# A two-layer decoder step on one core: the first FFN product by Strassen's seven products, each FFN in two phases through DRAM

## The chip, the cores and the metric

The kernel runs on one core of one Trainium2 chip. The time is device microseconds of one execution. Lower is better. Three runs of the kernel before took 2004.39, 2007.34 and 2011.28 us, so the median is 2007.34 us.

## The reference

One inference step works on 1024 prompt tokens, 16 meta tokens ahead of them, and 8 sample tokens: 1048 columns of 1024 features, in float32. Layer 0 mixes by causal pooling, layer 1 by sliding-window attention. After each mixer stands a layer norm, then the ConvFFN, then a layer norm:

```python
gu = xs @ w_in                       # 1024 -> 2 x 2816: gate and up
g, u = gu[..., :D_FF], gu[..., D_FF:]
gp = concatenate([prefix, g], axis=1)
c = conv_b + sum(gp[:, k:k + S] * conv_w[k] for k in range(3))
h = silu(c) * u
return h @ w_out, gp[:, -2:]         # 2816 -> 1024
...
hp = layer_norm(ALPHA * hp + f_p, g, b)
```

## The kernel before

Features lie on the 128 partitions and tokens along the columns. The tokens come in three chunks of 280, 384 and 384 columns (in layer 1 the first chunk has 266 for the gate and 264 elsewhere, since most meta tokens are no longer needed). Every float32 operand of a product is split into a high part and a low part, `h` or `hi` and `l` or `lo`, and `mm3` (L115 to L122) adds three products of parts: hi by hi, hi by lo, lo by hi. A layer norm (`ln_steps`) ends by writing the two parts of its result: ScalarE writes the high part `xh`, and VectorE the low part `xl` at L233 (POOL at L222 for some tiles). `load_w` (L103 on) fetches a weight tile by a DMA on the SP queue, casts it on ScalarE (L111) and subtracts on POOL for the low part (L112).

The FFN (`ffn`) runs over 22 feature tiles f of the inner width. For each tile and each chunk `ffn1` makes the gate `pg` and the up value `pu` in one PSUM bank each, 24 matmuls a bank (8 feature tiles k times three parts). POOL, VectorE and ScalarE then make the convolution, the Silu, the product and the two parts of h, which stay in SBUF. After every second f, `ffn2` multiplies two h tiles with their output weights, 8 output tiles of 6 matmuls, and VectorE adds each bank to the accumulator `acc` (L420). `ffn2_last` does this for the last two tiles (L433, L441). Layer norms of early chunks run beside the products of later ones, both at the FFN's end and at its start, where the FFN of chunk 0 begins while chunk 2 is still in the mixer's norm.

The program is traced in source order; a scheduler orders each engine's instructions by priority and by when they are ready, and sets the waits. Six PSUM banks turn under the name "mm". The mean of a norm is a product with `ones` (L143, or L165 and L166 after sums on POOL and VectorE), the subtraction is L188, the scaling by gain and inverse deviation L224. In the pooling L326 adds a product to the sum; in the attention's output projection it is L762 and L764, where `pz` is the product of 12 matmuls for each half.

Of the kernel before, what the change touches and what calls it, by code (L numbers as in the profile page):

```python
# [13 lines left out]
P = 128  # L14
D = 1024
KT = D // P
SEQ = 1024
# [10 lines left out]
# prompt blocks (of 128 tokens) per chunk; the first chunk also carries the  # L28
# meta tokens and the sample tokens: columns [meta 16 | samples 8 | prompt]
# [6 lines left out]
# columns alive after the attention: [meta14 meta15 | samples 8 | prompt]  # L36
# [3 lines left out]
# packed per-partition constant columns  # L40
# [7 lines left out]
# constants of the first phase alone  # L48
# [9 lines left out]

@with_exitstack
def trunk_kernel(ctx: ExitStack, tc: tile.TileContext, ins: dict, outs: dict):  # L60
    nc = tc.nc
    pool = ctx.enter_context(tc.tile_pool(name="sb", bufs=1))
    psum = ctx.enter_context(tc.tile_pool(name="ps", bufs=1, space=bass.MemoryType.PSUM))

    def bank(name, tag="mm"):
        return psum.tile([P, 512], F32, tag=tag, bufs=6 if tag == "mm" else 2, name=name)

    def tmp(shape, name, dt=F32):
        return pool.tile(shape, dt, tag="tmp", bufs=8, name=name)

    def ltmp(shape, name, dt=F32):
        return pool.tile(shape, dt, tag="lt", bufs=5, name=name)

    def tiny(shape, name):
        return pool.tile(shape, F32, tag="tiny", bufs=6, name=name)

    def hslot(shape, name, dt=F32R):
        return pool.tile(shape, dt, tag="h", bufs=12, name=name)

    # ------------------------------------------------------------ constants  # L80
# [7 lines left out]
    cr = pool.tile([P, NF, NCH, 2], F32, name="carry")  # L88
    gs = pool.tile([P, NF, NS], F32, name="gs")
# [3 lines left out]

    def xh_tile(c, m, name, dt=F32R):
        return pool.tile([P, WX[c]], dt, tag=f"xh{c}_{m}", name=f"{name}{c}_{m}")

    xh = [[xh_tile(c, m, "xh") for m in range(KT)] for c in range(NCH)]
    xl = [pool.tile([P, KT, WX[c]], F32R, name=f"xl{c}") for c in range(NCH)]
# [4 lines left out]
    def load_w(src, name, tag="w", pieces=1, w=None):  # L103
        raw = pool.tile([P, 1024], F32, tag="raw", bufs=2, name=f"raw_{name}")
        nc.sync.dma_start(raw, src)
        if w is None:
            w = pool.tile([P, 2, 1024], F32R, tag=tag, bufs={"w": 4, "wo": 2}.get(tag, 1), name=f"w_{name}")
# [7 lines left out]
    def mm3(out, wts, movs):  # L115
        """out += sum_k w_k^T x_k over exact hi/lo parts (all but lo*lo)."""
# [859 lines left out]
```

## Time and profile before

| | us |
|---|---|
| median of three runs | 2007.34 |
| the runs | 2004.39, 2007.34, 2011.28 |
| span of the profiled execution | 2004.4 |
| TensorE busy in it (PE) | 1932.9 (96%), 12208 matmuls |
| VectorE (DVE) | 1263.3 (63%) |
| ScalarE (ACT) | 712.3 (36%) |
| POOL | 813.9 (41%) |
| DMA moved | 123.45 MB |

The durations that the profile gives for matmuls overlap, since matmuls are pipelined: a listed 0.33 us is the time of one from its start to its end, and the distance between starts is what a stream of them costs. PEclk is the granted TensorE clock as a share of full speed.

### The profile page before, as it was taken

The numbers are of one execution on the slowest core, as the hardware profiler recorded it, in microseconds if no ns is written. First come the engines' busy times: TensorE is split into PE (matmuls) and PEld (weight loads), VectorE is DVE, ScalarE is ACT, GpSimd is POOL, SyncE is SP. The second block draws the span as 40 slices with busy tenths as digits, with TensorE's granted clock in tenths as the row PEclk, the third lists the DMA queues.
The fourth block names the chain that finished last, engine by engine and source line by source line (L and its number), as shares of the span: only waits on it lengthen the run. The fifth ranks groups of instructions, "written<-read, shape, count | busy, mean of one in ns | idle before, by whom it ended". The sixth has DMA issues, their size and how long they took to land. (4 is left out here: it accounts for less than half of the span.)

```text
span 2004.4 us, 31349 instructions
## 1 busy us (share of the span) xinstructions
PE 1932.9 (96%) x12208; PEld 1896.3 (95%) x12208; DVE 1263.3 (63%) x2367; ACT 712.3 (36%) x1585; POOL 813.9 (41%) x880
## 2 busy tenths in 40 slices
PE   6899999999999999899999989999999999999997
PEld 4699999999999999889999988999999999999996
DVE  7977545454544456887989896675445454544566
ACT  2452122112211221476778784512122112212234
POOL 6752334214321432653464657533143224322333
PEclk9899999999999999999999999999999999999998
DMA  5201111101110111314343322011011011101102
GB/s 194 78 22 43 53 54 63 43 22 64 64 37 27 64 53 34 30 49 148 107 132 102 109 81 85 32 51 55 33 64 55 31 42 63 54 32 43 64 23 65
DMA packets 50422, 123.45 MB, mean 62 GB/s; under 512 B 11481, under 2 KB 25489, under 8 KB 50217
## 3 DMA queue, kind: packets, MB, share of 16 engines
q1 hardware_dynamic: 50272, 121.44, 19.6%
q8 instruction: 96, 1.57, 0.3%
q14 instruction: 54, 0.43, 0.1%
HBM read 108.29 MB, written 7.54 MB: 58 GB/s over the span
## 5 line engine op out<-in xcount | busy, mean ns | idle before, releaser
L112 POOL TENSOR_TENSOR w_wo<-raw_wo,w_wo 128x512 fp32r<-128x512 f32 (+1 forms) x92 | 169.3, 1859 | 550.9 <-ACT w_wo L111 548.0
L121 PE MATMUL pg<-xl,w_g 128*128 128x384 f32 (+2 forms) x1056 | 337.4, 319 | 0.0
L121 PE MATMUL pu<-xl,w_u 128*128 128x384 f32 (+2 forms) x1056 | 336.6, 319 | 0.0
L420 DVE TENSOR_TENSOR acc<-acc,po 128x384 f32<-128x384 f32 (+2 forms) x432 | 222.1, 515 | 173.8 <-PE po L122 170.9
L121 PE MATMUL po<-h,w_wo 128*128 128x384 f32 (+2 forms) x960 | 305.9, 319 | 0.0
L120 PE MATMUL po<-h,w_wo 128*128 128x384 f32 (+2 forms) x960 | 305.7, 318 | 0.0
L122 PE MATMUL po<-h,w_wo 128*128 128x384 f32 (+2 forms) x960 | 305.6, 318 | 0.0
L111 ACT CAST w_wo<-raw_wo 128x512 fp32r<-128x512 f32 (+1 forms) x92 | 71.6, 822 | 422.4 <-PE po L122 417.6
L402 DVE TENSOR_TENSOR h<-c,h 128x280 fp32r<-128x280 f32 (+2 forms) x132 | 147.7, 1119 | 88.3 <-ACT h L401 87.7
L392 POOL TENSOR_SCALAR c<-g,cols 128x384 f32<-128x384 f32 (+1 forms) x110 | 80.2, 729 | 294.6 <-issue 281.6
L121 PEld LDWEIGHTS pg<-xl,w_g 128*128 128x128 f32 x1056 | 198.8, 188 | 0.1
L121 PEld LDWEIGHTS pu<-xl,w_u 128*128 128x128 f32 x1056 | 198.3, 188 | 0.0
L393 DVE SCALAR_TENSOR_TENSOR c<-g,cols,c 128x384 f32<-128x384 f32 (+1 forms) x110 | 67.8, 616 | 194.4 <-POOL c L392 194.4
L122 PEld LDWEIGHTS po<-h,w_wo 128*128 128x128 f32 x960 | 180.4, 188 | 0.0
L120 PEld LDWEIGHTS po<-h,w_wo 128*128 128x128 f32 x960 | 180.3, 188 | 0.0
L121 PEld LDWEIGHTS po<-h,w_wo 128*128 128x128 f32 x960 | 180.1, 188 | 0.0
L398 ACT ACTIVATE c<-c 128x280 f32<-128x280 f32 (+2 forms) x132 | 65.1, 493 | 312.4 <-DVE c L394 277.5
L120 PE MATMUL pg<-xh,w_g 128*128 128x384 f32 (+1 forms) x528 | 170.1, 322 | 0.0
L122 PE MATMUL pg<-xh,w_g 128*128 128x384 f32 (+1 forms) x528 | 169.1, 320 | 0.0
L120 PE MATMUL pu<-xh,w_u 128*128 128x384 f32 (+1 forms) x528 | 168.9, 320 | 0.0
L122 PE MATMUL pu<-xh,w_u 128*128 128x384 f32 (+1 forms) x528 | 168.8, 320 | 0.0
L120 PE MATMUL pg<-xa,w_g 128*128 128x384 f32 (+1 forms) x528 | 168.6, 319 | 0.0
(270 smaller groups left out, 4673.5 us busy)
## 6 DMA issues: line engine op xcount, KB each, us to landing
raw_g<-in_win SPq DMA_DIRECT2D x44, 512.0 KB, 3.5
raw_u<-in_win SPq DMA_DIRECT2D x44, 512.0 KB, 3.5
raw_wo<-in_wout SPq DMA_DIRECT2D x44, 512.0 KB, 3.5
raw_wq<-in_wq SPq DMA_DIRECT2D x24, 512.0 KB, 3.5
raw_wo<-in_wo SPq DMA_DIRECT2D x24, 512.0 KB, 3.6
q<-q SPq DMA_DIRECT2D x64, 96.0 KB, 2.1
praw<-in_xq SPq DMA_DIRECT2D x8, 400.0 KB, 5.4
out_yT<-acc SPq DMA_DIRECT2D x8, 384.0 KB, 2.5
```

The costliest lines, as they stand in the source:

```text
L111: nc.scalar.copy(w[:, 0, s], raw[:, s])
L112: nc.gpsimd.tensor_tensor(w[:, 1, s], raw[:, s], r32(w[:, 0, s]), ALU.subtract)
L120: nc.tensor.matmul(out, lhsT=wh, rhs=mh, start=(k == 0), stop=False)
L121: nc.tensor.matmul(out, lhsT=wh, rhs=ml, start=False, stop=False)
L122: nc.tensor.matmul(out, lhsT=wl, rhs=mh, start=False, stop=(k == n - 1))
L392: nc.gpsimd.tensor_scalar(cc, g[:, 0:n], w0, b, ALU.mult, ALU.add)
L393: nc.vector.scalar_tensor_tensor(cc, g[:, 1:1 + n], w1, cc, ALU.mult, ALU.add)
L398: nc.scalar.activation(ct, ct, AF.Silu)
L402: nc.vector.tensor_tensor(ht[:, 1, :], ct, r32(ht[:, 0, :]), ALU.subtract)
L420: nc.vector.tensor_tensor(a, a, ps, ALU.add)
```

## The change

Strassen's scheme (in the form with seven products and fifteen additions) takes the first FFN product. The weight block is two tiles f by two halves of the 1024 features, the token block two feature halves by two column quarters. Seven products of sums replace eight. `ffn_a` builds the seven token operands X once for each of two column halves b (quarters of 262 columns in layer 0, and of 260 in layer 1 with six dummy columns), each split into two parts. For each of 22 sets (11 pairs of f, gate then up) `prep` loads two weight tiles, makes four sums, and splits seven operands. Three accumulators of two banks each, B, A and C, take the products; the running values of B are copied out by ScalarE between the products that are added to it. Gate rows G, the convolution C and up rows U hold all tokens of a pair; h is written to DRAM. `ffn_b` then reads h and the residual back and does the second product in groups of three tiles f, with the layer norms behind it. All chunks' inputs are needed before the first set is complete. Memory is handed over in phases: pools are closed and opened between the stages. The attention's norm writes its scaled result to the new buffers of layer 1 in place of the parts of x.

```diff
-    def ffn(L, first_w):
...
-        win = {0: first_w, 1: load_in(1), 2: load_in(2, "wo")}
-        for c in range(NCH):
-            for f in range(3):
-                ffn1(f, c, *win[f])
...
+    def ffn_a(L, Y):
+        def build_x(b):
+            q = 2 * b * w
+            B = {(i, j): Y[i][:, :, q + j * w:q + (j + 1) * w] for i in range(2) for j in range(2)}
+            def parts(n, srcs, pool_lo):
+                t = lt.tile([P, 2, 4, w], F32R, tag=f"x{b}{n}", name=f"x{L}_{b}{n}")
+                for h, src in enumerate(srcs):
...
+                    nc.scalar.copy(t[:, 0, ks], src)
+                    (nc.gpsimd if pool_lo else nc.vector).tensor_tensor(t[:, 1, ks], src, r32(t[:, 0, ks]), ALU.subtract)
...
+        def prep(s):
+            raw = lt.tile([P, 2, 1024], F32, tag="raw2", bufs=2, name=f"raw{L}_{s}")
+            nc.sync.dma_start(raw, ins["win"][L, f:f + 2].rearrange("a p c -> p a c"))
+            def parts(n, src, eng):
+                t = lt.tile([P, 2, 512], F32R, tag="ws", bufs=8, name=f"w{L}_{s}{n}")
+                nc.scalar.copy(t[:, 0], src)
+                eng.tensor_tensor(t[:, 1], src, r32(t[:, 0]), ALU.subtract)
...
+            parts("11", A[0, 0], nc.gpsimd)
+            parts("12", A[0, 1], nc.vector)
+            nc.vector.tensor_tensor(st["s1"], A[1, 0], A[1, 1], ALU.add)
+            nc.vector.tensor_tensor(st["s2"], st["s1"], A[0, 0], ALU.subtract)
+            parts("s2", st["s2"], nc.gpsimd)
...
+        def prod(out, W, n, xn, start, stop, bs=(0, 1)):
+            for b in bs:
+                o = out[:, b, :w]
+                for k in range(4):
+                    nc.tensor.matmul(o, lhsT=wh, rhs=xh_, start=(start and k == 0), ...)
+                    nc.tensor.matmul(o, lhsT=wh, rhs=xl_, ...)
+                    nc.tensor.matmul(o, lhsT=wl, rhs=xh_, ...)
...
+        for s in range(NSET):
+            if s + 1 < NSET:
+                W[s + 1] = prep(s + 1)
+            A = ps.tile([P, 2, 512], F32, tag="st2", bufs=4, name=f"A{L}_{s}")
+            prod(A, W[s], "12", "21", True, True)
+            put_first(rows[0], u, lambda o, b, xs: nc.vector.tensor_tensor(o, A[:, b, xs], p1[:, b, xs], ALU.add))
+            prod(B, W[s], "s2", "t2", False, True)
+            u2 = pc(f"u2_{L}_{s}")
+            nc.scalar.copy(u2, B[:, :, :w])
+            C = ps.tile([P, 2, 512], F32, tag="st2", bufs=4, name=f"C{L}_{s}")
+            prod(C, W[s], "s3", "t3", True, True)
+            prod(B, W[s], "s1", "t1", False, True)
+            u4 = pc(f"u4_{L}_{s}")
+            nc.scalar.copy(u4, B[:, :, :w])
+            put_second(rows[1], lambda o: nc.vector.tensor_tensor(o, C[:, :, :w], u4, ALU.add))
+            if s + 1 < NSET:
+                first(s + 1)
+                first_copy(s + 1)
+            prod(B, W[s], "s4", "22", False, True)
+            put_second(rows[0], lambda o: nc.scalar.copy(o, B[:, :, :w]))
+            prod(C, W[s], "22", "t4", False, True)
+            put_first(rows[1], u, lambda o, b, xs: nc.vector.tensor_tensor(o, C[:, b, xs], u2[:, b, xs], ALU.add))
+            if u:
+                finish_h(p)        # U *= G's convolution, three DMAs to hd[L]
+            else:
+                conv(p)            # ScalarE, VectorE twice, ScalarE (Silu), for two rows
...
+    def ffn_b(L):
+        NG = 3
+        groups = [list(range(f, min(f + NG, NF))) for f in range(0, NF, NG)]
+        def load(f):
+            hr = lt.tile([P, TW], F32, tag="raw", bufs=3, name=f"hr{L}_{f}")
+            nc.sync.dma_start(hr[:, :cs[-1]], hd[L][f, :, :cs[-1]])
+            nc.scalar.copy(h[:, 0, :n], hr[:, :n])
+            nc.vector.tensor_tensor(h[:, 1, :n], hr[:, :n], r32(h[:, 0, :n]), ALU.subtract)
+            return h, load_w(ins["wout"][L, f], f"wo{L}_{f}", "wo", bufs=2 * NG, raws=3)
...
+        for c in range(NCH):
+            nc.sync.dma_start(acc[c], yd[L][:, :, x0 + cs[c]:x0 + cs[c + 1]])
...
+        for gi in range(len(groups)):
+            for c in range(NCH):
+                product(gi, c)
+                if gi == len(groups) - 1 and c:
+                    for _ in ln(c - 1):
+                        pass
```

## Rows read from the trace of the kernel before

**Rows 1.** Stretches: length, busy PE, PEld, DVE, ACT, POOL, granted clock, DMA share, GB/s.
```profile
0.00:82.50 82.50, 59.17 (x170) 36.86 (x171) 70.64 (x135) 28.64 (x55) 51.67 (x52) 0.90 0.49 164
82.50:849.00 766.50, 757.48 (x4758) 755.85 (x4757) 435.66 (x675) 196.56 (x378) 278.52 (x305) 1.00 0.14 44
849.00:889.00 40.00, 35.01 (x255) 33.62 (x254) 36.21 (x58) 27.61 (x59) 22.43 (x21) 0.99 0.22 56
889.00:1217.00 328.00, 311.55 (x2165) 305.53 (x2166) 293.37 (x840) 253.30 (x700) 175.47 (x214) 0.97 0.36 108
1217.00:1240.00 23.00, 22.70 (x151) 22.21 (x151) 6.84 (x14) 8.09 (x12) 18.60 (x15) 1.00 0.23 76
1240.00:1982.00 742.00, 739.24 (x4696) 738.41 (x4696) 407.17 (x627) 186.70 (x361) 262.31 (x273) 1.00 0.14 46
1982.00:2004.40 22.40, 7.76 (x23) 3.79 (x21) 13.44 (x22) 11.43 (x22) 4.90 (x4) 0.77 0.58 141
```

**Rows 2.** TensorE's waits: total us, times, longest.
```profile
PE po L433 <- DVE acc L441: 5.2, 2, 2.8
```

**Rows 3.** TensorE in order of time: start, duration, line, tile, shape; ends of three streams.
```profile
299.75 0.33 PE L121 MATMUL po<-h,w_wo 128*128 128x384 f32 x1
...
312.40 0.33 PE L122 MATMUL po<-h,w_wo 128*128 128x384 f32 x1
...
879.26 0.40 PE L577 MATMUL pv<-w_wv,xh 128*128 128x256 f32 x2
...
880.68 0.28 PE L577 MATMUL pv<-w_wv,xh 128*128 128x256 f32 x1
...
1459.96 0.28 PE L120 MATMUL pu<-xa,w_u 128*128 128x264 f32 x1
...
1462.77 0.29 PE L122 MATMUL pu<-xa,w_u 128*128 128x264 f32 x1
```

**Rows 4.** VectorE in order of time at the start of layer 0.
```profile
74.75 3.44 DVE L233 SCALAR_TENSOR_TENSOR xl<-zp,cols,xh 128x280 fp32r<-128x280 f32 x3
...
79.16 1.33 DVE L233 SCALAR_TENSOR_TENSOR xl<-zp,cols,xh 128x280 fp32r<-128x280 f32 x3
80.42 1.13 DVE L326 SCALAR_TENSOR_TENSOR zp<-pp,cols,zp 128x384 f32<-128x384 f32 x2
...
103.46 3.80 DVE L188 TENSOR_TENSOR zp<-zp,ps_mum 128x384 f32<-128x384 f32 x8
...
120.10 4.79 DVE L224 SCALAR_TENSOR_TENSOR zp<-zp,cols,rstd_m 128x384 f32<-128x384 f32 x6 [1.63 <-ACT rstd_m L201]
```

**Rows 5.** Groups of instructions by shape: busy us, mean ns, idle before and its releaser.
```profile
L111 ACT CAST w_g<-raw_g 128x1024 fp32r<-128x1024 f32 x44 | 46.3, 1052 | 71.1 <-DMA raw_g<-in_win 64.9 <-PE pz L122 6.2
...
L112 POOL TENSOR_TENSOR w_wo<-raw_wo,w_wo 128x512 fp32r<-128x512 f32 x48 | 63.0, 1331 | 32.2 <-ACT w_wo L111 29.4 <-issue 2.6
...
L661 DVE TENSOR_TENSOR ring<-tp,ring 128x512 fp32r<-128x512 f32 x64 | 44.0, 688 | 6.1 <-ACT ring L660 5.2
...
L660 ACT CAST ring<-tp 128x512 fp32r<-128x512 f32 x64 | 37.5, 586 | 17.9 <-PE tp L658 16.5
...
L111 ACT CAST w_wo<-raw_wo 128x512 fp32r<-128x512 f32 x48 | 27.4, 617 | 4.8 <-PE pz L122 3.6 <-DMA raw_wo<-in_wo 0.9
```

**Rows 6.** POOL and VectorE in order of time around 247 us.
```profile
245.21 4.75 POOL L112 TENSOR_TENSOR w_wo<-raw_wo,w_wo 128x1024 fp32r<-128x1024 f32 x2 [26.44 <-ACT w_wo L111]
...
247.61 2.38 DVE L397 SCALAR_TENSOR_TENSOR c<-gs,cols,pre 128x8 f32<-128x8 f32 x1 [2.80 <-ACT gs L375]
```

**Rows 7.** DMA issues of the page: count, size of each, median us to landing.
```profile
raw_wo<-in_wout SPq DMA_DIRECT2D x44, 512.0 KB, 3.5
```

**Rows 8.** VectorE in order of time at the start of layer 1's FFN.
```profile
1234.28 0.55 DVE L764 TENSOR_TENSOR z<-z,pz 128x384 f32<-128x384 f32 x1 [1.56 <-PE pz L122]
...
1246.06 3.79 DVE L188 TENSOR_TENSOR z<-z,ps_mum 128x384 f32<-128x384 f32 x8
...
1263.99 1.91 DVE L224 SCALAR_TENSOR_TENSOR y_m<-z,cols,rstd_m 128x384 f32<-128x384 f32 x2 [3.18 <-ACT rstd_m L201]
```

More of the change, by code (lines that the diff above doesn't have):

```diff
@@ L243, in pool_raw, with big @@
+    def big(name, shape=(P, 4, ROW), dt=F32):
+        return now["r"].tile(list(shape), dt, tag="big", bufs=2, name=name)
+    now["ps"] = Phase(tc, "ps0", None, bass.MemoryType.PSUM)
+    now["r"] = Phase(tc, "r0", "right")
+    now["l"] = Phase(tc, "l0", "left")
     def pool_raw(c, g):
@@ L250, in trunk_kernel @@
     W0 = HALO + NMETA + WP[0]
-    raw0 = pool.tile([P, KT, W0], F32, tag="acc1", name="raw0")
+    raw0 = now["l"].tile([P, KT, W0], F32, name="raw0")
+    ys0 = [big(f"y0_{i}") for i in range(2)]
     pw = [hslot([P, 2, 2, P], f"pw{g}", F32) for g in range(4)]
@@ L336, in pool_chunk, with cvc @@
             next(r, 0)
-        return z
+        return [zz[m // 4][:, m % 4, :] for m in range(KT)]
+    def cvc(L, j, f):
+        return C_CV + (L * 4 + j) * NF + f
     def cvc(L, j, f):
@@ L504, in ffn, with ln @@
-        nc.sync.dma_start(outs["ncp"][L], cr[:, :, NCH - 1, :])
-        nc.sync.dma_start(outs["ncs"][L], gs)
-    first = None
+        def ln(c):
+            z = [acc[c][:, m, :] for m in range(KT)]
+            o0 = 0 if c == 0 else NS + BLK0[c] * P
+            end = L == 1 and c == NCH - 1
+            if L == 1:
+                fin = fin_out(z, 3, outs["yT"][:, :, o0:o0 + UW[c]], acc[c], (6, 7), end)
+            else:
+                xh[c] = [xh_tile(c, m, "xh") for m in range(KT)]
+                xl[c] = now["x"].tile([P, KT, WX[c]], F32R, tag=f"xl{c}", name=f"xl{c}")
+                fin = fin_x(z, 1, c, (6, 7))
+            return ln_steps(z, UW[c], 2 * L + 1, c, f"f{L}{c}", fin, on_pe=end, lnexp=True, split=True,
+                            sq_tmp=hslot if end else None, pairs=end)
@@ L519, in trunk_kernel @@
     nc.gpsimd.tensor_scalar(nsink, nsink, -1.0, None, ALU.mult)
-    ffn(0, first)
+    now["ps"].close()
+    now["l"].close()
+    now["l"] = Phase(tc, "lA0", "left")
+    ffn_pre(0)
+    ffn_a(0, ys0)
+    now["l"].close()
+    now["r"].close()
+    now["ps"] = Phase(tc, "psB0", None, bass.MemoryType.PSUM)
+    now["r"] = Phase(tc, "rB0", "right")
+    now["x"] = Phase(tc, "x", "left")
+    now["l"] = Phase(tc, "lB0", "left")
+    ffn_b(0)
+    now["l"].close()
     nc.sync.dma_start(outs["npp"], ins["xtail"])
@@ L854, in trunk_kernel @@
             ji += 1
-    first = None
     while ji < len(jobs):
@@ L865, in trunk_kernel @@
             pass
-    ffn_pre(1)
-    ffn(1, first)
+    now["r"].close()
+    now["r"] = Phase(tc, "rA1", "right")
+    ys1 = [big(f"y1_{i}") for i in range(2)]
+    for t in ys1:
+        nc.gpsimd.memset(t[:, :, :DUM[1]], 0.0)
+    X0 = DUM[1]
+    for c in range(NCH):
+        n = WX[c] - (MOFF if c == 0 else 0)
+        tgt = [ys1[m // 4][:, m % 4, X0:X0 + n] for m in range(KT)]
+        for m in range(KT):
+            g, b = gain(2, m)
+            nc.scalar.activation(tgt[m], za[c][m], AF.Identity, bias=b, scale=g if m in SCALED else 1.0)
+        for i in range(2):
+            nc.sync.dma_start(yd[1][:, 4 * i:4 * i + 4, X0:X0 + n], ys1[i][:, :, X0:X0 + n])
+        X0 += n
+    now["ps"].close()
+    now["l"].close()
+    now["x"].close()
+    now["l"] = Phase(tc, "lA1", "left")
+    ffn_pre(1)
+    ffn_a(1, ys1)
+    now["l"].close()
+    now["r"].close()
+    now["ps"] = Phase(tc, "psB1", None, bass.MemoryType.PSUM)
+    now["r"] = Phase(tc, "rB1", "right")
+    now["l"] = Phase(tc, "lB1", "left")
+    ffn_b(1)
+    now["l"].close()
+    now["r"].close()
+    now["ps"].close()
 _OUTS = {
```

434 lines of the change are left out of this document (237 added, 197 removed).

## The prediction

> **What bounds the kernel now.** I read the span cut by stages first [rows 1], because a mean over the span hides them. The reader is to see two long stretches, 82.5 to 849 and 1240 to 1982, in which TensorE is busy 757 of 766 and 739 of 742 us at full granted clock, with VectorE near 57% and POOL near 36%. These are the two FFNs; TensorE bounds them. Between them lies the attention (889 to 1217), where VectorE is busy 293 of 328 us. The first 82.5 us, the 40 us after 849 and the last 22.4 us are layer norms and the pooling: short chains over VectorE, ScalarE and POOL. Second, the waits: the largest sum that TensorE has on an FFN's own results is 5.2 us in two waits [rows 2], so no wait is there to be won. Third, the spacing of matmul starts, not their listed durations, which overlap. From the first to the last row of each pair [rows 3], 73 steps at 384 columns take 12.65 us (0.1733 each), 23 steps at 264 take 2.81 (0.1222), 12 at 256 take 1.42 (0.118). The slope is 0.000426 us a column, so 0.0097 us of each matmul's time does not go away with its columns.
>
> **The product itself.** Before, each of 22 tiles f issues, for gate and up, 24 matmuls per chunk. Layer 0: 48 x (0.1290 + 2 x 0.1733) = 22.83 us, times 22 = 502.2 (0.1290 interpolated for 280). Layer 1, with 266 and 264 columns in chunk 0: 24 x (0.1231 + 0.1222) + 96 x 0.1733 = 22.52, times 22 = 495.5. After, a set makes 7 products x 2 halves x 4 k x 3 parts = 168 matmuls, 22 sets a layer: 3696 where there were 3168. Columns fall to 7/8, instructions rise by 1/6. At 262 columns (0.1213, between the 256 and the 264 rows) layer 0 takes 448.3; at 260 (0.1205) layer 1 takes 445.4. Saved: 53.9 + 50.1 = 104 us, not the 125 that an eighth would be. With 0.118 as the lower and 0.1222 as the upper price of one matmul the saving lies between 94 and 125. The second product keeps its 1584 matmuls: 251.1 and 247.5. 502.2 + 251.1 = 753 in a stretch of 766.5, 743 in one of 742: the spacing explains the stretches.
>
> **Start of layer 0.** Before, the FFN of chunk 0 begins at 82.5 while chunk 2 is still normalised. After, each product needs token quarters of all chunks. Chunk 2's sum is ready at 81.5 [rows 4]; the x-lo operations (3.44 + 1.33 us for chunk 0) leave VectorE, so 77. Then its mean needs seven POOL additions and a product, about 9 without the weight splits that sat there, and from its subtraction to its last scaling before took 21.4 (103.46 to 124.9): complete at 107.4. One half of X is built under this; TensorE then follows the other half part by part, loses some 4 us and 2 to a cold clock, but had the first block of 2.9 us before: effective start 109.5 for 82.5. Bounds: 98 if the chain runs as tightly as its own operations, 125 if it ends as before.
>
> **Inside phase A.** A set lasts 168 x 0.1213 = 20.4 us, a product 2.9. The other engines, per set [rows 5]: ScalarE seven 512-wide casts (4.3), four PSUM copies of 524 columns at 0.60 (2.4), half a pair's four 1040-wide activations (2.1): 8.8. VectorE seven 512-wide at 0.69 (4.8), evacuations (three of 524 columns in all, cut into some nine pieces) 3.1, half a pair's four convolution steps of 1040 columns at an estimated 1.4 and two short ones 3.1, half of two products 1.2: 12.2. POOL four 512-wide at 1.33: 5.3. None reaches 20.4, so nothing replaces TensorE as the bound on average. But the accumulators are tied: after s2 ScalarE must copy B before s1 may add to it, one product later; the same after s1 and after s4. Of 2.9 us the copy takes 0.6 [rows 5] and its signals some 0.3, and 2.0 is left for whatever stands before it on ScalarE. Behind that copy queue the casts of the next weights and the Silu; ahead of it may stand a Silu or a cast that waits for VectorE. Rows show how late VectorE can be: an operation on 8 columns took 2.38 us while POOL's subtraction ran [rows 6]. The page "SBUF — State Buffer" of the Trainium skill (Who interferes with whom) says why: a VectorE instruction with two SBUF inputs waits for the whole of a POOL instruction that reads SBUF. By that rule VectorE needs up to 12.2 + 5.3 = 17.5 of a set's 20.4; without it 12.2; what it would cost is the first rival. The trace of before has no such tied accumulator. Bounds: 0 a set (slack holds; an added wait can't give time back) and 2.4 (one VectorE operation late by a POOL operation, once a set), that is 0 to 53 a layer. I take 0.7 a set, 15 a layer, nearer to 0, because in the FFNs of before, where ScalarE and VectorE evacuate every bank too, TensorE idles 9 of 766 and 3 of 742 us [rows 1].
>
> **A to B.** h goes to DRAM and back, by SP's queue alone, which gets some 40 issues more a layer; what counts of them is the order. The write of the last pair and its reading are off the path (tiles 20 and 21 are the last group). On the path: the first group needs three h and three weight tiles of some 0.5 MB, each 3.5 us to land [rows 7], through three raw buffers on one SP queue, each then cast on ScalarE (1.05 [rows 5]) and split on VectorE (1.4, twice the 512-wide row) or POOL (2.4 [rows 6]). Their places in SBUF come free as X and the last evacuations release them: part lands early, part after the end. I take 11 us idle. Least 5 (one load and one split after the end), most 20 (all six behind the last write: 3.5 for it, 3.5 for the first, five more at an estimated 2.7). The loads of acc from DRAM, 4.3 MB, have six banks' time (7 us) plus the gap; taken as hidden, up to 5 if not.
>
> **Layer 0 in sum.** 109.5 + 448.3 + 15 + 11 + 251.1 = 834.9 against 849: -14.1.
>
> **Into the attention.** Before, chunk 0 was normalised by then and chunk 1 half. After, the last group has one tile (5.6, 7.7, 7.7 us per chunk), so chunk 0's norm starts only 15 us before the end; key, value and query products of chunk 0 wait for it. 36 of the 40 us are VectorE [rows 1], and it gains about 10 more, hidden partly in the 15: +3 (0 to +15). The attention is the same; the x-lo work of two chunks' norms leaves VectorE, eight operations of about 0.6, so 5 us, counted next. The copies of state rows to outputs move behind the first FFN, where nothing waits for them.
>
> **Start of layer 1.** Before, FFN products run beside chunk 2's output projection and norm; effective start 1982 - 743 = 1239. After, the eight projection tiles run alone (12 x 0.1733 each), done at 1231, 1226 with the 5. Before, 29.7 us pass from its last sum over the subtraction of the mean to the first scaling [rows 8], with FFN work and weight splits between; I take 17.5, the chain's own operations, then 5 for scaling: 1248.5; with X, clock and first block as above 1253: +14 (+5 to +26).
>
> **Layer 1 and end.** -50.1 + 15 + 11 = -24.1. The last norm took 22.4 us with the others done [rows 1]; now chunk 1's runs beside it: +6 (+2 to +16).
>
> **Sum.** -14.1 + 3 + 14 - 24.1 + 6 = -15. The profiled span is 2004.4, equal to the lowest of the three runs, so nothing lies around it; their median is 2007.3. Forecast 2007.3 - 15 = 1992. Differences within 0.3% (6 us) count as none.
>
> **Rivals.** (1) Slower: ScalarE's copies of B come late. For: 2.0 us of slack three times a set, VectorE held up by POOL, one queue in order. Against: mean loads of 43 and 60%. It decides from 1.2 us a set (0.7 plus 22/44, the forecast's 15 and the margin of 6, spread over 44 sets). At 2 us a set it adds 44 x 1.3 = 57: 2049. (2) No change: the gaps are 20 each, because all loads of the first group stand on SP behind the last pair's write, which waits for VectorE's product: 2 x 9 more, 2010. For: one queue in order. Against: tiles 0 to 2 of h are written 10 pairs earlier, and some of the space they go to is free 3 to 15 us before the end. (3) A larger gain: no stall, gaps of 5: 30 + 12 less, 1950. For: the mean loads. Against: the tied accumulators and the full stop at each seam. (4) The saving is not made, because a matmul of 262 columns costs as much as a bigger one: at the mean spacing of before (502.2 / 3168 = 0.1585) 3696 would take 586, 84 more a layer, so 2175. Against it stand the rows of 256 and 264 columns [rows 3], so I give it no chance.
>
> **Chances.** Forecast case (1965 to 2001): 0.47. Rival 1: 0.28. Rival 2: 0.13. Rival 3: 0.12. So faster 0.59, same 0.13, slower 0.28. The range for 8 in 10 reaches half into rival 3 and over most of rival 1: 1955 to 2042; the likeliest case's own range is 1965 to 2001.
>
> **What would show it.** Right: matmul spacing 0.121 in phase A; a set of about 21 us; TensorE's first X product near 105 to 110; two idle gaps of about 11 us between the phases; waits of TensorE on ScalarE's u2 and u4 copies of some 30 us in sum. Wrong: a spacing above 0.125, waits on those copies or on weight splits above 60 us, gaps over 20, or a first FFN product after 125.

## The result, and the profile after

The changed kernel takes 2128.8 us (median of 4 runs, 2126.4 to 2131.2), the kernel before on the same chip 2009.1: ratio 1.0601, interval 1.0579 to 1.0622. It is slower by 120 us, where I had forecast 15 us less; the time lies outside my range. One execution, of e13_two_sets below, took 2700.8 us at a granted clock of 0.645 over its whole span (0.95 in its neighbours), and nothing is concluded from it.

The profiled span is 2128.3. First the stretches of the changed kernel, cut where its phases meet; columns as in [rows 1].

```profile
0.00:104.30 104.30, 57.88 (x164) 34.80 (x164) 80.84 (x152) 38.55 (x77) 54.83 (x60) 0.82 0.38 129
104.30:157.00 52.70, 22.13 (x136) 21.05 (x137) 49.89 (x49) 23.34 (x43) 35.21 (x23) 0.64 0.20 63
157.00:592.00 435.00, 434.31 (x3562) 433.95 (x3561) 235.71 (x414) 183.20 (x274) 135.73 (x92) 1.00 0.26 72
592.00:611.00 19.00, 9.42 (x52) 8.49 (x52) 7.46 (x8) 6.34 (x6) 7.13 (x3) 0.82 0.95 310
611.00:857.50 246.50, 246.50 (x1538) 246.32 (x1536) 125.64 (x214) 39.61 (x39) 52.20 (x23) 1.00 0.30 98
857.50:959.00 101.50, 44.04 (x268) 38.95 (x267) 69.76 (x106) 48.52 (x98) 50.02 (x44) 0.68 0.12 35
1306.00:1380.00 74.00, 26.45 (x134) 23.23 (x134) 61.85 (x62) 33.95 (x62) 52.79 (x38) 0.58 0.18 67
1380.00:1806.60 426.60, 424.95 (x3522) 424.54 (x3520) 237.17 (x393) 180.56 (x272) 134.06 (x92) 1.00 0.24 73
1806.60:1831.00 24.40, 15.64 (x95) 14.91 (x96) 8.54 (x9) 8.17 (x8) 6.14 (x3) 0.72 1.08 236
1831.00:2075.60 244.60, 243.88 (x1540) 243.55 (x1539) 123.65 (x214) 39.36 (x39) 55.20 (x26) 1.00 0.29 94
2075.60:2128.30 52.70, 14.51 (x33) 7.26 (x31) 33.13 (x58) 25.84 (x55) 20.05 (x21) 0.65 0.23 80
```

The long stretches are as good as hoped: 3562 matmuls in 434 us (0.122 each), TensorE without a gap, at full clock, in both layers. The loss lies in four short stretches in which TensorE is busy 28 to 43% of the time, at a granted clock of 0.58 to 0.68: 104 to 157, 857 to 959, 1306 to 1380, 2076 to the end. [rows 1] shows two of their forerunners, 40.0 us after the first FFN and 22.4 us at the end.

To follow them through all kernels I use six points of each trace: the start of the last Strassen product of layer 0 (end A0), of the last matmul of layer 0's second FFN product (last po), of the first score product of the attention, of the last output-projection product (pz), of the last Strassen product of layer 1, of the last po matmul of layer 1. "Seam" is last po to first score, "start 1" is last pz to end A1 less the 445.4 us of products that my forecast gave, "tail" is last po to the end.

| kernel | end A0 | last po | first score | seam | last pz | end A1 | start 1 | last po | tail | span |
|---|---|---|---|---|---|---|---|---|---|---|
| before | | 848.3 | 883.9 | 35.6 | 1233.9 | | | 1981.1 | 23.2 | 2004.4 |
| after | 591.8 | 857.4 | 956.5 | 99.1 | 1302.5 | 1812.3 | 64.4 | 2075.6 | 52.6 | 2128.3 |
| e1 | 590.0 | 864.0 | 944.3 | 80.3 | 1287.6 | 1797.4 | 64.4 | 2065.0 | 35.0 | 2100.0 |
| e2 | 592.0 | 863.5 | 939.3 | 75.8 | 1282.9 | 1796.1 | 67.8 | 2062.8 | 45.8 | 2108.6 |
| e3 | 583.8 | 848.8 | 948.3 | 99.5 | 1289.7 | 1790.6 | 55.5 | 2053.1 | 51.5 | 2104.6 |
| e7 | 579.4 | 847.0 | 927.9 | 80.9 | 1274.4 | 1780.6 | 60.8 | 2043.0 | 40.9 | 2083.9 |
| e9 | 577.9 | 847.0 | 908.7 | 61.7 | 1262.2 | 1772.0 | 64.4 | 2033.9 | 40.9 | 2074.8 |
| e12 | 572.3 | 841.4 | 906.0 | 64.6 | 1261.4 | 1765.1 | 58.3 | 2033.6 | 35.3 | 2068.9 |
| e14 | 572.5 | 841.2 | 904.2 | 63.0 | 1259.8 | 1754.8 | 49.6 | 2020.8 | 35.1 | 2055.9 |
| e8, no statistics | 591.1 | 861.0 | 915.2 | 54.2 | 1261.1 | 1771.1 | 64.6 | 2034.4 | 15.5 | 2049.9 |
| e16, no statistics | 573.7 | 843.2 | 875.5 | 32.3 | 1216.5 | 1711.5 | 49.6 | 1977.5 | 6.5 | 1984.0 |
| e17, before, no statistics | | 841.9 | 873.8 | 31.9 | 1218.5 | | | 1960.2 | 13.5 | 1973.7 |

Before against after: last po of layer 0 comes 9.1 us later in spite of the cheaper product, the seam is 63.5 longer, first score to last pz 4.0 shorter, last pz to last po of layer 1 25.9 longer (773.1 for 747.2), the tail 29.4 longer: 123.9 in all.

Inside the seam, in order of time (VectorE, ScalarE and TensorE of the changed kernel):

```profile
867.03 5.76 DVE L269 SCALAR_TENSOR_TENSOR acc<-acc,cols,rstd_f 128x280 f32<-128x280 f32 x6 [0.51 <-ACT rstd_f L218]
889.39 5.57 DVE L269 SCALAR_TENSOR_TENSOR acc<-acc,cols,rstd_f 128x384 f32<-128x384 f32 x6
912.81 4.83 DVE L269 SCALAR_TENSOR_TENSOR acc<-acc,cols,rstd_f 128x384 f32<-128x384 f32 x6 [1.95 <-ACT rstd_f L218]
...
919.54 1.99 ACT L135 CAST w_wk<-raw_wk 128x1024 fp32r<-128x1024 f32 x2
...
920.63 0.60 PE L144 MATMUL pk<-xh,w_wk 128*128 128x280 f32 x1 [9.03 <-ACT w_wk L135]
```

The three chunks' last steps of the norm stand 22 to 23 us apart, one norm behind the other, and only then are the key weights cast. Chunk 0's x was ready at 877; its first key product starts at 920.6. VectorE is busy for most of this row of norms, 38 of the 46 us between the first and the third of these steps (columns as above):

```profile
867.03:912.81 45.78, 5.41 (x8) 2.30 (x8) 38.14 (x55) 21.72 (x44) 25.18 (x24) 0.50 0.00 0
```

Before, the same steps stood 42 and 30 us apart (VectorE of the kernel before). The first came 38 us ahead of the last po (848.3), the third beside the key, value and query products of the chunks that were done, and TensorE was busy 35 of the 40 us from 849 [rows 1]:

```profile
810.59 3.67 DVE L224 SCALAR_TENSOR_TENSOR acc<-acc,cols,rstd_f 128x280 f32<-128x280 f32 x6
...
852.54 5.63 DVE L224 SCALAR_TENSOR_TENSOR acc<-acc,cols,rstd_f 128x384 f32<-128x384 f32 x6 [0.82 <-ACT rstd_f L201]
...
882.35 4.66 DVE L224 SCALAR_TENSOR_TENSOR acc<-acc,cols,rstd_f 128x384 f32<-128x384 f32 x6
```

At the start of layer 0, ScalarE's first casts of X, then VectorE and POOL:

```profile
104.30 5.39 ACT L448 CAST x<-y 128x524 fp32r<-128x524 f32 x10
...
106.11 1.80 DVE L458 TENSOR_TENSOR t<-y,t 128x524 f32<-128x524 f32 x1
107.83 3.33 DVE L449 TENSOR_TENSOR x<-y,x 128x524 fp32r<-128x524 f32 x2
111.09 1.60 DVE L488 TENSOR_TENSOR s<-raw 128x512 f32<-128x512 f32 x1
112.72 1.68 DVE L489 TENSOR_TENSOR s<-s,raw 128x512 f32<-128x512 f32 x1
...
106.06 9.31 POOL L449 TENSOR_TENSOR x<-y,x 128x524 fp32r<-128x524 f32 x6 [1.90 <-ACT x L448]
115.33 1.73 POOL L449 TENSOR_TENSOR x_0t<-t,x_0t 128x524 fp32r<-128x524 f32 x1
```

No part of X is cast before chunk 2's norm is complete, at 104.4. Operations of VectorE that take 0.69 us alone [rows 5] take 1.6 to 1.8 beside POOL's. TensorE waits meanwhile (total, times, longest; 95 to 200 us):

```profile
PE B L506 <- ACT w L480: 17.9, 1, 17.9
PE A L508 <- DVE w L481: 12.5, 1, 12.5
PE C L506 <- ACT x_0t L448: 4.7, 1, 4.7
```

### The profile page after: what moved, and what is told of

The parts are those of the page before. It is cut to its first block, busy times and chain, and to the rows that moved or that the text cites. A ratio compares the mean times of both kernels' runs of the same rounds, so it can differ in the third digit from the quotient of the medians.

```text
span 2128.3 us, 33727 instructions
## 1 busy us (share of the span) xinstructions
PE 1867.9 (88%) x13264; PEld 1819.0 (85%) x13264; DVE 1322.8 (62%) x2507; ACT 875.9 (41%) x1659; POOL 773.7 (36%) x633
## 4 chain that ended last, share of the span: by engine, by line
PE 77%; DVE 12%; ACT 3%; POOL 3%; DMA 2%; issue 2%; SPq 0%; DVEq 0%; POOLq 0%; ACTq 0%
PE B L506 8%; PE B L508 8%; PE B L507 8%; PE po L146 7%; PE po L144 7%; PE po L145 7%; PE C L507 4%; PE C L508 4%; PE C L506 4%; PE pq L785 3%; PE A L506 2%; PE A L507 2%; PE A L508 2%; PE pv L755 1%; PE av L854 1%
## 5 line engine op out<-in xcount | busy, mean ns | idle before, releaser
L144 PE MATMUL po<-hh,w_wo 128*128 128x384 f32 (+2 forms) x1056 | 342.3, 325 | 17.0 <-ACT w_wo L135 10.7
L145 PE MATMUL po<-hh,w_wo 128*128 128x384 f32 (+2 forms) x1056 | 340.1, 323 | 0.0
L146 PE MATMUL po<-hh,w_wo 128*128 128x384 f32 (+2 forms) x1056 | 334.9, 322 | 2.0 <-POOL w_wo L136 2.0
L645 DVE TENSOR_TENSOR acc<-acc,po 128x384 f32<-128x384 f32 (+2 forms) x336 | 164.4, 512 | 185.2 <-PE po L146 184.8
L481 POOL TENSOR_TENSOR w<-raw,w 128x512 fp32r<-128x512 f32 x88 | 131.9, 1500 | 314.7 <-ACT w L480 310.1
L144 PEld LDWEIGHTS po<-hh,w_wo 128*128 128x128 f32 x1056 | 200.8, 190 | 18.6 <-ACT w_wo L135 18.4
L145 PEld LDWEIGHTS po<-hh,w_wo 128*128 128x128 f32 x1056 | 201.0, 190 | 0.0
L146 PEld LDWEIGHTS po<-hh,w_wo 128*128 128x128 f32 x1056 | 198.0, 190 | 2.7 <-POOL w_wo L136 2.7
L506 PE MATMUL B<-x,w 128*128 128x262 f32 (+1 forms) x352 | 102.3, 291 | 37.5 <-ACT w L480 37.5
L549 DVE TENSOR_TENSOR U<-U,G 128x1048 f32<-128x1048 f32 (+1 forms) x44 | 65.8, 1494 | 97.7 <-ACT U L598 97.6
L480 ACT CAST w<-raw 128x512 fp32r<-128x512 f32 x132 | 81.7, 621 | 79.5 <-PE C L508 47.6
L508 PE MATMUL A<-x,w 128*128 128x262 f32 (+1 forms) x352 | 101.8, 289 | 13.6 <-DVE w L481 13.6
L626 DVE TENSOR_TENSOR hh<-hr,hh 128x1048 fp32r<-128x1048 f32 (+1 forms) x44 | 76.2, 1733 | 47.9 <-ACT hh L625 47.9
L506 PE MATMUL A<-x,w 128*128 128x262 f32 (+1 forms) x352 | 101.6, 289 | 0.0
L508 PE MATMUL B<-x,w 128*128 128x262 f32 (+1 forms) x352 | 101.5, 288 | 0.0
L507 PE MATMUL A<-x,w 128*128 128x262 f32 (+1 forms) x352 | 101.4, 288 | 0.0
L507 PE MATMUL B<-x,w 128*128 128x262 f32 (+1 forms) x352 | 101.4, 288 | 0.0
L506 PEld LDWEIGHTS B<-x,w 128*128 128x128 f32 x352 | 68.2, 194 | 38.6 <-ACT w L480 38.6
```

The lines of the kernel that those rows point to most:

```text
L144: nc.tensor.matmul(out, lhsT=wh, rhs=mh, start=(k == 0), stop=False)
L145: nc.tensor.matmul(out, lhsT=wh, rhs=ml, start=False, stop=False)
L146: nc.tensor.matmul(out, lhsT=wl, rhs=mh, start=False, stop=(k == n - 1))
L480: nc.scalar.copy(t[:, 0], src)
L481: eng.tensor_tensor(t[:, 1], src, r32(t[:, 0]), ALU.subtract)
L506: nc.tensor.matmul(o, lhsT=wh, rhs=xh_, start=(start and k == 0), stop=False, skip_group_check=True)
```

## The experiments

Theory after this reading: the loss is at the seams, in three parts: norms no longer covered by products; the attention's weights and memory, handed over only after the norms; operands made at the start of phase A by engines that hinder each other. Rivals: two phases cost as such whatever the product (e4), or Strassen's operands are all of it. Where no number of runs is given, a variant ran once, on one of several chips; the kernel before spread from 2001.5 to 2011.8 us over all its runs, so totals less than some 6 us apart are not told from each other, and stages are read from the traces.

**e1.** The last two groups chunk by chunk, the single tile first.
```
-groups = [list(range(f, min(f + NG, NF))) for f in range(0, NF, NG)]
+groups = [[0]] + [list(range(f, f + NG)) for f in range(1, NF, NG)]
+# last two groups: for c: product(G-2, c); product(G-1, c); then ln(c - 1)
```


> Theory (the time is lost where the phases meet, here because the last group of the second product is one inner tile, so that 24 products of a chunk cover little of a norm): with the last six inner tiles taken chunk by chunk, some 23 us of products stand behind each of the first two norms. The tail after the last po product goes from 53 us to 24 to 30, the stretch from the last po of layer 0 to the first attention unit from 102 to 60 to 75; total 2128 to about 2070. Rival (the norms are slow because VectorE and GpSimd are held by something else than their place in the order): tail stays over 45, total 2110 to 2130.

2101.8 us, in neither range. The tail fell to 35.0, but the seam only to 80.3: half of what I expected. The K and V weights still followed the last norm (first key product at 908.1, last po 864.0).

**e2.** K and V weights in a ring beside the accumulators, cast ahead of the last groups; NG = 2.
```
-NG = 3
+NG = 2
+if gi + 2 == len(groups) and L == 0: wk, wv = load_w(...)
```


> Groups of two inner tiles make room for the K and V weights beside the second product. Theory (K/V projections start at 920 because their weights are cast only after all three norms): first K product right after the first norm's output, near 880, first attention unit near 920 to 930 instead of 959; the tail gets 4 to 8 us shorter from the longer last group; total about 2085 to 2095. Rival (the three norms themselves keep K/V back): first unit stays after 950 and the total above 2115.

2110.4: between the two. The first key product came at 868.3, as the theory said, but the first score only at 939.3. The weights were one wait, another stood behind it.

**e3.** All low parts and differences of the right operand on VectorE.
```
-(nc.gpsimd if pool_lo else nc.vector).tensor_tensor(t[:, 1, ks], ...)
+nc.vector.tensor_tensor(t[:, 1, ks], ...)
```


> All sixteen GpSimd subtractions of the right operand's blocks go to VectorE, 11 us more of its work at 0.69 us each. Theory (VectorE and GpSimd slow each other: 1.6 to 1.8 us for operations that take 0.69 alone): steady products begin some 10 us sooner in each layer (157 to about 147, 1380 to about 1370), total about 2105 to 2112. Rival (VectorE's amount of work is the limit, without a loss from GpSimd): some 11 us later in each layer, total about 2150.

2106.4: end A0 8.0 sooner, start 1 8.9 shorter. Giving VectorE 11 us more work made it quicker.

**e4.** Two phases, eight plain block products.
```
+for i, j: prod(C, W, f"{i+1}1", f"1{j+1}", True, False); prod(C, W, f"{i+1}2", f"2{j+1}", False, True)
```


> Two phases as in the changed kernel, but the first product as eight block products, with four right and four left blocks instead of seven. Theory (the meeting of the phases costs, whichever product is made): product phase 64 us longer per layer (513 for 449), start of each layer 10 to 20 us shorter for want of the sums, the other seams as they were: about 2215 to 2235. Rival (making the operands of Strassen's form is most of the loss): both starts as short as in the kernel before, total 2150 to 2170.

2206.0, a little under the theory's range. Seam and tail are as in the changed kernel (99.4 and 51.3). Phase A of layer 0 ends 40.6 us later (632.4), where the eighth product alone is some 61 by the spacings of these traces (4224 matmuls at 0.1212 for 3696 at 0.1221; 62 in layer 1). So the seven-product form gives 77 us in all, net of some 20 us a layer for its extra operands. Two phases without it lie 196 us over the kernel before, of which some 23 are the plain product itself in narrower matmuls (512 and 509 us for 502.2 and 495.5).

**e5.** Twelve temporaries for the norms, NG = 2.
```
-tag="lt", bufs=5
+tag="lt", bufs=12
```


> Groups of two inner tiles as in e2_kv_early (K and V weights stay late), and twelve temporaries for the norms in place of five outside the attention. Theory (back-to-back norms stand in line for the five temporaries: in e2_kv_early their outputs come 25 us apart while VectorE has some 16 us of work for one): outputs 16 to 18 us apart, tail after the last po from 45.8 us (e2_kv_early) to 32 to 37, total about 2095 to 2103. Rival (each norm is held by its own chain from engine to engine, whatever the memory): outputs still 22 to 25 us apart, tail over 43, total 2118 to 2126.

2120.4, tail 45.9: my theory fell. The outputs came 22 to 23 us apart, as in the changed kernel with its five, so the number of temporaries holds nothing back. That the chain from engine to engine does, as the rival has it, is not shown either: VectorE was busy 38.1 of the 45.7 us between the first and the third (864.9 to 910.6), 19 us a norm and not some 16.

**e6.** First half of layer 0's right operand in memory of its own, over e3.
```
+now["xa"] = Phase(tc, "xA0", "right")
+build_x(0, ys0, 0, X0, now["xa"], now["l"])   # ahead of the pooling phase's release
```


> As e3_x_vector (2106 us), and the first half of layer 0's right operand is made in memory that the pooling phase does not use, ahead of the release of that phase's tiles. Theory (the operands of columns 0 to 523 are ready after chunk 1, but wait for the memory of the pooling phase): they fill VectorE's gaps beside chunk 2 (80.8 of 104 us busy), first products near 105 to 108, steady ones some 12 to 16 us sooner than in e3_x_vector, total 2090 to 2095. Rival (VectorE has no gaps that long there, chunk 2 is pushed back by as much): total 2103 to 2110.

2100.5, end A0 580.7 for 583.8: 3 us of the 12 to 16. The rival is nearer: X was begun at 65.2, and chunk 2's norm was complete 10 us later than in e3 (112.6 for 102.5).

**e7.** Operands as in e6, the last groups as in e1 with two tiles, temporaries as in e5, one weight ring.
```
-w = now["l"].tile([P, 2, 1024], F32R, tag=tag, bufs=bufs, name=f"w_{name}")
+w = now["w"].tile([P, 2, 1024], F32R, tag="w", bufs=4, name=f"w_{name}")   # now["w"] = rB0
```

> All of it: operands on VectorE and the first half early (as e6_x_early), groups of two inner tiles with the last two groups chunk by chunk, twelve temporaries, and one ring of four weight tiles shared by the second product and the attention, so that K and V weights follow the last output weights. Theory (four separate waits at four places, so the gains add up except between norms and K/V): total about 2035 to 2055, the first attention unit 65 to 75 us after the last po of layer 0 in the changed kernel becomes 45 to 55, tail 24 to 30. Rival (the gains hide one another, one seam stays as long as its longest part): above 2070.

2085.7: the rival. The tail fell to 40.9 for 24 to 30. The seam stayed at 80.9, because of this (POOL and ScalarE of e7; KS is the attention's tile of keys):

```profile
907.21 0.31 POOL L736 MEMSET KS<- 128x256 f32 x1
...
911.30 1.28 ACT L752 ACTIVATE KS<-pk,cols 64x256 fp32r<-64x256 f32 x3
```

The key products had begun at 848.7, and KS was first written at 907, right behind POOL's last use of the last norm's reciprocal root (905.0 to 907.3).

**e8.** The changed kernel without the statistics of the norms behind the second product.
```
-return ln_steps(z, UW[c], 2 * L + 1, c, ...)
+nc.vector.tensor_scalar(rstd, z[0], 0.0, 1.0, ALU.mult, ALU.add); return fin(rstd)
```


> The changed kernel, with the mean and the variance left out of the two norms behind the second product (three chunks each): the products with gain, the split and the output stay. Theory (three norms, one behind the other, stand open behind a last group of one inner tile): the first attention unit, 99 us after the last po in the changed kernel, comes 45 to 60 us after it, the tail falls from 53 to 20 to 28 us, total 2050 to 2065. Rival (K and V weights and the handing over of memory take the time whatever the norms do): first unit over 75 us after the last po, total above 2090.

2051.7: as the theory said, but for the tail, 15.5.

**e9.** The norms' temporaries, five again, with the accumulators and no longer under KS, over e7.
```
-return now["l"].tile(shape, dt, tag="lt", ...)
+return (now.get("n") or now["l"]).tile(shape, dt, tag="lt", bufs=5, ...)   # now["n"] = rB0
```


> As e7_combined (2086 us), but the norms' temporaries lie with the accumulators (five, kept through the attention) and no longer under the keys and queries of the attention's own phase. In e7_combined the first copy of a finished K product into KS starts at 911, 43 us after that product, at the end of the last norm. Theory (memory handed over from the last norm's temporaries holds the attention's start): copies of K begin right behind their products, the first attention unit moves from 928 to 905 to 912, total 2062 to 2072. Rival (priority of the norms or the queue order holds it): first unit within 5 us of 928, total 2080 to 2090.

2076.6. The mechanism is right, first score at 908.7 (928 before) and KS written here (ScalarE of e9):

```profile
867.76 0.46 ACT L751 ACTIVATE KS<-pk,cols 64x256 fp32r<-64x256 f32 x1
```

The total missed its range by 5 us: from the first score to the last pz took 7 us longer than in e7, and start 1 was 3.6 longer. That the attention, begun sooner, shared VectorE with the last norm would explain the 7, but no run shows it.

**e10.** Groups of three again, with two raw buffers for three to make room, over e9.
```
-bufs=3, name=f"hr{L}_{f}"
+bufs=2, name=f"hr{L}_{f}"
```


> As e9_norm_memory with groups of three inner tiles again, the single one first, so that six tiles (23 us of products a chunk, for 16) are taken chunk by chunk at the end. Theory (a norm is hidden as far as products of the next chunk stand behind it): tail 41 us in e7_combined becomes 33 to 36 as in e1_b_last (35.0), first attention unit a further 4 to 8 us sooner, total 10 to 15 us under e9_norm_memory. Rival (the last norm's own chain is the whole tail): no more than 4 us under e9_norm_memory.

2091.4, slower than e9. The tail did fall to 34.8, but each second product, from its first to its last po, took 18 to 19 us longer: TensorE's waits in e10, 590 to 860 us (1.5 us in e9 on that line):

```profile
PE po L144 <- ACT w_wo L135: 10.1, 3, 4.0
PE po L144 <- DVE acc L646: 3.6, 1, 3.6
```

The edit took from the loads more than it gave the norms.

**e11.** Two small POOL instructions taken from the starts, over e9.
```
-nc.gpsimd.memset(G[:, 0:2, 0:2], 0.0)      # now after the first sums
-ffn_pre(0); ffn_pre(1)                      # now beside chunk 2 and in the attention
```


> As e9_norm_memory (2077 us), with two GpSimd instructions taken out of the starts of the product phases: the memset of two columns of G (issued after the first sums of row pair 0, on VectorE) and the four small products of the convolution's state (made beside chunk 2 of the pooling and in the attention). In e9_norm_memory the first weight subtraction of each layer stood behind them in GpSimd's queue: PE waited 9.4 us in layer 0 (G still held as Y) and 10.6 us in layer 1, where a product of 0.48 us took 13.73 us while VectorE ran without a gap. Theory (GpSimd's queue in order, and GpSimd shut out by VectorE): both waits fall below 3 us, total 2057 to 2064. Rival (the operands on VectorE are what the products would wait for next, at the same time): each start gains less than 4 us, total above 2068.

2077.2: nothing gained, my theory failed as stated. In layer 0 the wait of 9.4 us became one of 8.7, in layer 1 that of 10.6 one of 11.7 on the next POOL subtraction (TensorE's waits of e11, layer 1, 1258 to 1400 us):

```profile
PE B L508 <- ACT w L482: 26.9, 1, 26.9
PE B L510 <- POOL w L483: 11.7, 1, 11.7
```

**e12.** The first set's left operands on VectorE, layer 1's Y in the accumulators' memory, three tiles a group in layer 1, over e11.
```
+(eng if s else nc.vector).tensor_tensor(t[:, 1], ...)
+now["w"] = now["n"] = Phase(tc, "rW0", "right")
```


> As e11_pool_queue, and: the first set of left operands wholly on VectorE; layer 1's Y written in the accumulators' memory, half on VectorE and half on ScalarE, as soon as a chunk's norm is done; the second half of layer 1's right operand under x, so that the rest does not wait for the last norm; groups of three inner tiles in layer 1, the last two chunk by chunk. Theory (what is left at the start of layer 1 is the writing of Y, 16 us, behind the last norm, and the memory it waits for; the tail is the products that stand behind each norm): layer 1 starts 12 to 20 us sooner, the tail falls from 41 to 33 to 36 us, total 2030 to 2042, still above the kernel before. Rival (VectorE's operand work sets the start whatever the memory): total 2050 to 2062.

2070.5 (2068.7 to 2074.0, 4 runs), ratio to before 1.0308, 1.0286 to 1.0330, above both ranges. The tail came as expected (35.3), and end A0 8.4 us sooner than in e11; start 1 gained 5 us for 12 to 20. Against this, end A1 to the last po took 6.6 us longer with three tiles a group, and seam and attention together 5.6. Why start 1 gained no more (POOL, then VectorE of e12, in order of time):

```profile
1305.82 12.58 POOL L483 TENSOR_TENSOR w<-raw,w 128x512 fp32r<-128x512 f32 x1 [23.10 <-ACT w L482]
1318.37 1.27 POOL L483 TENSOR_TENSOR w_1s<-s,w_1s 128x512 fp32r<-128x512 f32 x1
...
1305.67 0.68 DVE L442 TENSOR_TENSOR x_0t<-t,x_0t 128x520 fp32r<-128x520 f32 x1
...
1316.61 0.67 DVE L496 TENSOR_TENSOR s<-raw,s 128x512 f32<-128x512 f32 x1
1323.38 0.69 DVE L483 TENSOR_TENSOR w_1s<-s,w_1s 128x512 fp32r<-128x512 f32 x1 [6.10 <-ACT w_1s L482]
```

One subtraction of 1.27 us lasted 12.58, until VectorE's row without a gap had ended at 1317.3.

**e13, e15.** The second set on VectorE too, over e12; the same kernel twice.
```
-(eng if s else nc.vector)
+(eng if s > 1 else nc.vector)
```


> As e12_best (2070 us), with the second set of left operands of each layer wholly on VectorE too. In e12_best the first GpSimd subtraction of layer 1, 1.27 us elsewhere, took 12.58 us (1305.8 to 1318.4), until VectorE's unbroken row of operations ended at 1317.3, and PE waited 9.8 us for it. Theory (GpSimd gets nothing done while VectorE runs operations on two fp32 operands without a gap): the wait goes, 2.4 us of VectorE's work comes in its place, 5 to 9 us less in layer 1 and 0 to 4 in layer 0, total 2057 to 2065. Rival (VectorE's own work is what the products reach next, as after e11_pool_queue): total 2067 to 2073.

> The same kernel as e13_two_sets, whose one execution ran at a granted clock of 0.6 to 0.7 from start to end (0.95 in its neighbours), so that its total says nothing. Theory (GpSimd is shut out while VectorE runs without a gap): 2059 to 2067. Rival (VectorE's own work is reached next): 2067 to 2073.

e15: 2060.7 (2 runs), 9.8 us less, of which 9.6 lie between the last pz and end A1. The wait for POOL is gone from TensorE's waits. With e11 this tells the two apart: the place in POOL's queue cost nothing by itself, being shut out did.

**e14.** The first half of layer 1's operand issued ahead of chunk 2's Y, over e13.
```
+if c == 2: build_x(1, ys1, 0, X1, now["xa"], now["l"])
```


> As e13_two_sets, and the first half of layer 1's right operand (columns 0 to 519, chunks 0 and 1 of Y) is issued ahead of chunk 2's Y, in memory of its own, as in layer 0. In e12_best its first cast starts at 1283.4, right behind ScalarE's last Y of chunk 2, though chunks 0 and 1 were normalised before. Theory (the order of issue holds it, and ScalarE and VectorE have 10 us or more free beside the last norm): steady products 8 to 14 us sooner, total 2046 to 2055. Rival (it delays the last norm on VectorE by as much as it saves): within 4 us of e13_two_sets.

2058.7 (4 runs), ratio 1.0271, 1.0242 to 1.0299: 2 us under e15, so the rival: chunk 2's Y was complete 29.4 us after the last pz, in e15 23.0. With e15, from which its total can't be told, it is the best version run, and still slower than the kernel before.

**e16, e17.** The edit of e8 on e14, and its like on the kernel before.

> As e14_x_first (2059 us), with mean and variance of the norms behind the second product left out, as in e8_no_stats. Theory (what is left over the kernel before is mostly the last norm of each layer, bare of products): the tail falls from 35 to 15 to 20 us, the first attention unit from 63 to 38 to 48 us after the last po, total 2015 to 2028, so that the form with free norms would still not be under the kernel before. Rival (norms are hidden by now and the attention's own preparation holds the seam): tail as above, first unit over 55 us after the last po, total 2030 to 2040.

> The kernel before with the same part left out as in e8_no_stats: mean and variance of the norms behind the second product. Theory (in the kernel before two of three norms lie beside products, so that little of them is bare): tail from 23 to 5 to 10 us, first attention unit from 36 to 25 to 32 us after the last po, total 1970 to 1985, 20 to 35 us less, where the changed kernel lost 78 us. Rival (the norms cost the kernel before as much, and the seams differ for another reason): total below 1945.

e16: 1985.8, 73 us less; I had expected 30 to 44, and seam (32.3) and tail (6.5) lie under the theory's ranges too. e17: 1975.5, in the range, but for the tail, 13.5 for 5 to 10. Without these statistics seam and tail shrink by 44.9 and 37.2 us in the changed kernel (e8), by 3.6 and 9.7 in the kernel before.

## Why the prediction was wrong

Right: the product. 0.122 us a matmul for the 0.1213 of the forecast, 448 us of products from an effective start of 143.5 (591.8 - 448.3). Right, or better than forecast: inside phase A the copies of B cost TensorE 0.7 us in layer 0 and 1.6 in layer 1, where I gave 15 a layer, and rival 1, with 0.28 the likeliest of the rivals, is refuted; ScalarE was busy 183 of 435 us and had the time. Right within 5 us, partly because two misses offset each other: the gap and the second product together, 265.6 and 263.3 us from end A to the last po, for 262.1 and 258.5. TensorE idled 9.6 and 8.8 us in the gaps (592 to 611, 1806.6 to 1831) for 11, and the second product took 5 and 7 us more than forecast. The gaps of 20 of rival 2 did not come.

Wrong: the four other seams. In the forecast's own terms, measured less forecast: start of layer 0 143.5 for 124.5 with its stalls (+19.0); gaps and second products +3.5 and +4.8; into the attention +63.5 for +3 (+60.5); the attention -4 for -8 (its last projection at 1226 for 1234; +4); last pz to end A1 64.4 us besides the products, for 27 (1226 to 1253) and 15 of stalls (+22.4); the end +29.4 for +6 (+23.4). Together 137.6 of the 138.9 us between the span and its forecast. The two starts were missed by more than this: the 15 us of stalls a layer did not come, and without them it is 143.5 for 109.5 and 64.4 for 27. That the stalls hid part of it was luck.

**Into the attention** is the step that failed most: "chunk 0's norm starts only 15 us before the end", "it gains about 10 more, hidden partly in the 15: +3 (0 to +15)". I took VectorE's 36 busy us of 40 [rows 1] for the measure of the stretch, gave it 10 more, and let the rest run as before. It gained 33.6: 69.8 busy us from 857.5 to 959. The norms that the kernel before had done beside products were now all to come, three in a row, 22 to 23 us each, of which some 19 are VectorE's and the rest its waits on the other engines. e8 and e17 price it: the seam loses 44.9 us without statistics in the changed kernel, 3.6 in the kernel before, so 41.3 of the 63.5 are norms that lost their cover. The other 22 are what I did not look for at all: weights and memory that pass to the attention by phase. e16, with both mended and no statistics, has a seam of 32.3, the kernel before without statistics 31.9; e8 has 54.2. e2 and e9 show the two parts of it, the K and V weights and KS under the norm's temporaries. One thing stays open: six scalings of 384 columns took VectorE 5.57 us in the bare norms and 3.25 in e8 (at 873.5); whether POOL's share of the statistics lengthens them, no run tested.

**The end** has the same cause: 37.2 us of statistics against 9.7, so 27.5 of the 29.4. The step "now chunk 1's runs beside it: +6" did not set the last group's 7.7 us of products a chunk, which the forecast had worked out, against a norm of more than 20. With 23 us of products a chunk (e1, e12) the tail is 35.

**The two starts**: "One half of X is built under this; TensorE then follows the other half part by part, loses some 4 us and 2 to a cold clock". The norm ahead of it was right: chunk 2's Y was complete at 104.4 for 107.4, and in layer 1 23.8 us after the last pz for 22.5. But nothing of X was cast under it; the casts begin at 104.30 and at 1326.15, right behind the last Y, and the effective start came 39 and 41 us after Y, where the forecast had 2.1 and 4.5. Its 4 and its 2 us had no row behind them. e6 and e14 built the first half early, in memory of its own, which pushed chunk 2's norm back by 10 and 6 us: of the 12 to 16 hoped for, 3 came in layer 0, and in layer 1 no more than the 2 that the totals can't tell.

In the row of operations behind Y, VectorE and POOL took turns: 1.6 to 1.8 us for 0.69. I had quoted the rule for this, but priced it only inside phase A, where it did no harm. Moving POOL's share to VectorE gave 8 to 9 us a layer (e3); keeping POOL out of the first set came with 8.4 more in layer 0 (e12 over e11), and out of the second with 9.6 in layer 1 (e15). With all this, end A0 lies 19.4 us under the changed kernel's in e12, as much as layer 0's +19.0. Some 20 us a layer are the cost of Strassen's extra operands in the changed kernel (e4); how much of them is this taking of turns, the runs do not say. In layer 1 what e3 had gained was gone again in e7 and e9 (start 1 60.8 and 64.4 for 55.5), for a cause that I did not find. What is left of start 1 in e14, 49.6 us, holds the last norm and VectorE's row of operations; I did not separate these further.

Of the saving of 104 us, then, the product gave what it should, within 5 us by its spacing (0.1221 and 0.1210 in the two layers). The price of everything beside it, which my sum set at 89 us (104 saved, 15 left over), was 228 (104 saved, 124 lost). Mended as far as the runs went, the form is 53 us slower than the kernel before (2058.7 and 2005.2 on one chip); without the norms' statistics on both sides the spans lie 10 us apart (1984.0 and 1973.7, one execution each).

The forecast's signs of being wrong did not give it away: spacing 0.122, the copies' waits 2.3 us in sum, those on the first sets' weights 56 at the two starts, gaps under 10, a first X product at 114.0. All of them look at the product phases, their first product and the gap between them; none stood at the way into the attention or at the end. In its working, 107.4 + 4 + 2 - 2.9 is 110.5 and not 109.5, the same terms on 1248.5 give 1251.6 and not 1253, and the 2175 of rival 4 leaves out the 89 us of the other terms; hardly anything of the miss hangs on these.

## What to carry to other kernels

When a change splits a pipelined stage in two, list for each boundary the work that used to lie beside products and now has none, and price all of it, with the waits between its engines: here 22 to 23 us a norm, 19 of them VectorE's. Look at which pool's memory the next stage's first tiles get, because a tile that overlaps the last temporaries starts after them whatever the queues say. And before a last group is cut, count the products that stand behind each closing step: here 7 us where a norm needs over 20.

## What the runs showed of the hardware

GpSimd (POOL) was held up far beyond one instruction of VectorE: while VectorE ran two-input fp32 operations without a gap, 18 in e12 and 21 in e9, a GpSimd subtraction of 1.27 us took 12.58 (e12), and a product of 0.48 us on 176 columns 13.73 (e9, 1299.9 us):

```profile
1299.91 13.73 POOL L416 TENSOR_TENSOR pre<-st,cols 128x176 f32<-128x176 f32 x1 [15.52 <-DMA st<-in_sc]
1313.61 0.48 POOL L418 TENSOR_TENSOR st<-st,cols 128x176 f32<-128x176 f32 x1
```

Once GpSimd was in, the two took turns, 1.6 to 1.8 us each (the changed kernel from 106 us, e9 from 1315). Which of the two it will be, no run tested. The Trainium skill, page "SBUF — State Buffer", section "SBUF: two separate sides", says of a VectorE operation with two SBUF inputs and a GpSimd operation that reads SBUF that whichever starts first gets the shared ports for its whole instruction, and the other fully blocks; the taking of turns agrees with it, and the 12.58 and 13.73 us, over many instructions, go beyond what it says.

TensorE's granted clock was 0.50, the lower of its two levels (1.2 of 2.4 GHz), while it had only the few products of a norm (1.3 us of 10 in e9, 1272 to 1282), and 1.00 through the product phases. In the seam of the changed kernel the key products ran 0.233 us apart from 923.9 until the clock rose at 927.2, and 0.129 apart after, so the low clock cost some 1.5 us there; what it cost at the other seams was not worked out.
